# One GpSimd operation ahead of the weight-sum DMAs of a hybrid decoder layer

## The chip, the core and the metric

The kernel runs on one core of a Trainium2 chip. A core has five engines that run their own instruction streams and meet only at semaphores: TensorE (PE in the profile; its weight loads are PEld), VectorE (DVE), ScalarE (ACT), GpSimd (POOL) and SyncE (SP). DMAs are issued from the streams of SP, ACT and POOL, and all of them are carried out by the same 16 DMA engines. The metric is the device time of one execution in microseconds, as the median of three runs.

## The reference

The reference is one inference step of one decoder layer, for a prompt of 2048 tokens and for 8 samples of 8 tokens, in float32. Cut to what matters here:

```python
proj = einsum('btd,dp->btp', x, w_in)              # 1024 -> 3584: q, f, i, g, B, C, h
qh   = silu(q)
f    = lb + (1 - lb) * sigmoid(f_pre)              # forget gate;  k = 1 - f
o    = hgrn2(qh, log f, k, i)                      # gated linear recurrence, 4 heads of 128
o    = o * rsqrt(mean(o * o) + 1e-6) * onorm_g * silu(g)
yc   = B * conv3(C * h)
x    = layer_norm(alpha * x + concat(o, yc) @ w_out)
hid  = square(relu(x @ w_ff1))                     # 1024 -> 4096
x    = layer_norm(alpha * x + hid @ w_ff2)         # 4096 -> 1024
```

The outputs are the tokens after the second norm, the final states of the recurrence and the last two rows of the convolution's input, for prompt and samples.

## The kernel before

**Tiling.** The prompt is worked in four blocks of 512 tokens (`for b in range(NB)`); the samples ride along in the second block. Each block goes through the same stages: `m1` (the projections of q and f for the four heads, eight units), `m2` (i and g, eight units), `m3` (the convolution's three projections, twelve units), the output projection, the first norm, `ff1` and `ff2`. A unit is one weight tile of 128 x 1024 float32, 512 KB. Every float32 product is made of three fast matmuls: a high part and a low part of both operands are kept, and `mm3` (lines 230 to 232) issues high x high, high x low and low x high. A unit of `m1` on 512 columns is therefore 8 x 3 = 24 matmuls of 128x512.

**Weights.** All weight tiles of the whole run stand in one list (`units`) in the order of use. `unit_dma` (lines 171 and 173) issues the load of the next one from SP, into a `tok` buffer for the first six units and into one of three `st` buffers afterwards. `unit_split` makes the high part on ACT (line 194, or 155 for halves) and the low part on DVE (line 201 or 156). The block's input `x` comes through the same list. In the first block the list begins: first tile of q (unit 1's weights), four tiles of `x`, first tile of f (unit 2's weights), second tile of q (unit 3's weights), and so on, so unit 1 needs five tiles in SBUF and each later unit one more. Before the loop six loads are issued, then the small constants, then seven tiles are split.

**m1.** `main()` is a generator that yields twice per unit. Odd units give q. Even units give f and k: ACT takes the sigmoids out of PSUM (lines 433, 434) and scales them (435, 437); the results are `fs[h]` and `ks[h]`. With these, `head(h)` later works on DVE, and it overwrites `ks[h]` in place (line 585).

**The weight sums.** `ff2` uses a fast matrix multiplication scheme with seven products in place of eight. For that it needs four sums and differences of quarters of `w_ff2`, called T1 to T4, for each of eight chunks. They do not depend on the input, and they are built in DRAM by DMAs issued from POOL: `make_sums` yields 64 DMAs of 512 KB, 32 plain copies (line 331) and 32 accumulating ones (line 329, the destination is read, added to and written). Consecutive steps on the same chunk wait for the DMA before them; with eight chunks in turn, up to eight are in flight. The results are first read by the loads of `ff2` in the first block (`st<-T`). The loop that drives `main()` calls `making` twice per step from step 8 on, in the first block only.

**What sets the order.** The kernel fixes the program order itself, and each engine runs its own part of it in order. The position in the program is therefore not a time: an instruction runs as soon as its engine's earlier instructions have been issued and its semaphores are there. On POOL nothing stands ahead of the sums but three small memsets; behind them come the small power operations of the first block's norms (line 686 for the recurrence's outputs, line 262 for the layer norm).

Of the kernel before, what the change touches and what calls it, by code (L numbers as in the profile page):

```python
# [13 lines left out]
ALU = mybir.AluOpType  # L14
AX = mybir.AxisListType

P = 128
# [36 lines left out]
def hybrid_step(ctx, tc, a, o):  # L54
    nc = tc.nc
    v, s, g, te = nc.vector, nc.scalar, nc.gpsimd, nc.tensor
# [8 lines left out]
    def new(shape, tag, bufs, dt=F32, of=None):  # L65
        count[0] += 1
        return (of or pool).tile(list(shape), dt, tag=tag, bufs=bufs, name=f"{tag}{count[0]}")
# [26 lines left out]
    def SM(shape):  # L94
        return new(shape, "sm", 16)
# [129 lines left out]
    def pump():  # L225
        if bg:
            bg.pop(0)()
# [147 lines left out]
    for b in range(NB):  # L375
# [20 lines left out]
        qs, ks, fs, scs, kds = {}, {}, {}, {}, {}  # L396
# [421 lines left out]
        def rec_step():  # L818
            nonlocal rec_done
            if not rec_done:  # L820
                rec_done = next(rec, 0) == 0

        def main():
            yield from m1()
            yield from m2()
            yield from m3()

        for i, _ in enumerate(main()):
            rec_step()
            if b == 0 and i >= 8:  # L830
                next(making, 0)
                next(making, 0)
            if i >= 16 and i % (3 if samp else 4) == 0:
                rec_step()
            if i % 2 == 0:
                pump()
# [445 lines left out]
```

## Time and profile before

| | before |
|---|---|
| median of 3 runs | 2435.18 us (2433.24 to 2436.19) |
| profiled execution | 2430.45 us, of which the span is 2428.6 us |
| PE busy | 2393.4 us (99%) |
| DVE / ACT / POOL busy | 1535.9 us (63%) / 1115.1 us (46%) / 132.4 us (5%) |
| DMA, moved in all | 358.78 MB, mean 148 GB/s |
| queue q1 (issued from SP) | 313.88 MB, 39.5% of the 16 engines' time |
| queue q0 (issued from POOL) | 42.54 MB, 6.6% |

The span runs from the first to the last instruction; the time of an execution is 1.85 us longer in the profiled one. A busy PE is not a PE at its peak: a matmul's end is modelled, so the distance between the starts of matmuls says more than busy time does. "Landing" of a DMA is when its semaphore comes; an ACT or DVE instruction that waits for it starts right then, so its start tells when the tile landed. The DMA share is the mean busy share of the 16 engines and can read a little over 1.

### The profile page before, as it was taken

To read this page: it belongs to the slowest core of one execution; us is meant where nothing else is said; L and a number is where in the kernel's file an instruction comes from. 1 tells how busy PE (TensorE), PEld (TensorE's weight loads), DVE (VectorE), ACT (ScalarE), POOL (GpSimd) and SP (SyncE) were. 2 spreads that over 40 slices of the span, in tenths; PEclk is the share of its full clock that TensorE was granted. 3 is DMA by queue.
4 is the path that set the end of the run, shared out by engine and by line. 5 is a ranking of instruction groups with operands and counts; after the bars stand their busy time and mean duration, and the time that the engine had idled before them with its cause. 6 is when DMAs were issued, how large, how long until landed. Compare 5 with 4: busy or idle time off the path is not lost.

```text
span 2428.6 us, 32948 instructions
## 1 busy us (share of the span) xinstructions
PE 2393.4 (99%) x12876; PEld 2050.9 (84%) x12876; DVE 1535.9 (63%) x2370; ACT 1115.1 (46%) x1794; POOL 132.4 (5%) x159
## 2 busy tenths in 40 slices
PE   7999999999999999999999999999999999999998
PEld 5888988888889889997878888988887888988886
DVE  5756822787865684227778856623887865832787
ACT  4334644555324455445554244544555324644553
POOL 3210000000001110000000000000000000000001
PEclk9999999999999999999999999999999999999999
DMA  9984433566223733234453325423565324433563
GB/s 326 279 240 174 157 104 113 170 188 210 79 77 77 210 125 105 82 102 152 161 190 105 100 74 196 145 99 118 186 207 166 104 76 163 156 113 103 169 195 114
DMA packets 103547, 358.78 MB, mean 148 GB/s; under 512 B 11552, under 2 KB 16032, under 8 KB 103392
## 3 DMA queue, kind: packets, MB, share of 16 engines
q1 hardware_dynamic: 91216, 313.88, 39.5%
q0 software_dynamic: 12032, 42.54, 6.6%
q8 instruction: 101, 1.65, 0.3%
q14 instruction: 54, 0.44, 0.1%
q10 hardware_dynamic: 144, 0.26, 0.0%
HBM read 345.59 MB, written 44.60 MB: 161 GB/s over the span
## 4 chain that ended last, share of the span: by engine, by line
PE 49%; DVE 2%; DMA 1%; issue 0%; ACT 0%; ACTq 0%; DVEq 0%; SPq 0%
PE ps L230 11%; PE ps L232 10%; PE ps L231 10%; PE ps L238 5%; PE ps L236 5%; PE ps L237 5%; PE ps L654 1%; DMA st<-T 1%; DVE wl L201 1%; PE ps L241 0%; PE ps L242 0%; DMA st<-in_w_ff 0%; DVE tok L1081 0%; PE ps L743 0%; PE ps L740 0%
## 5 line engine op out<-in xcount | busy, mean ns | idle before, releaser
L201 DVE TENSOR_TENSOR wl<-st,wh 128x1024 fp32r<-128x1024 f32 x514 | 627.8, 1222 | 500.6 <-ACT wh L194 499.8
L230 PE MATMUL ps<-X,wh 128*128 128x512 f32 (+2 forms) x2272 | 778.2, 343 | 15.7 <-ACT X L155 12.4
L232 PE MATMUL ps<-X,wl 128*128 128x512 f32 (+2 forms) x2272 | 768.0, 338 | 1.1 <-DVE wl L201 1.1
L231 PE MATMUL ps<-X,wh 128*128 128x512 f32 (+2 forms) x2272 | 768.2, 338 | 0.3 <-DVE X L156 0.3
L194 ACT ACTIVATE wh<-st 128x1024 fp32r<-128x1024 f32 x515 | 543.3, 1055 | 370.6 <-PE ps L238 155.2
L230 PEld LDWEIGHTS ps<-X,wh 128*128 128x128 f32 x2272 | 430.5, 189 | 61.3 <-ACT X L155 14.0
L232 PEld LDWEIGHTS ps<-X,wl 128*128 128x128 f32 x2272 | 430.4, 189 | 43.7 <-DVE wl L201 1.9
L231 PEld LDWEIGHTS ps<-X,wh 128*128 128x128 f32 x2272 | 430.6, 190 | 41.8 <-DVE X L156 2.4
L238 PE MATMUL ps<-wh,l 128*128 128x512 f32 x868 | 340.3, 392 | 2.8 <-DVE l L156 2.3
L237 PE MATMUL ps<-wl,h 128*128 128x512 f32 x868 | 338.5, 390 | 0.6 <-DVE wl L201 0.6
L236 PE MATMUL ps<-wh,h 128*128 128x512 f32 x868 | 338.3, 390 | 0.0
L1011 ACT ACTIVATE raw<-ps 128x256 f32<-128x256 f32 (+1 forms) x184 | 85.7, 466 | 371.2 <-PE ps L232 369.4
L238 PEld LDWEIGHTS ps<-wh,l 128*128 128x128 f32 x868 | 163.1, 188 | 43.9 <-DVE l L156 10.5
L237 PEld LDWEIGHTS ps<-wl,h 128*128 128x128 f32 x868 | 163.1, 188 | 36.2 <-DVE wl L201 2.2
L236 PEld LDWEIGHTS ps<-wh,h 128*128 128x128 f32 x868 | 163.2, 188 | 33.3 <-ACT h L155 0.3
L156 DVE TENSOR_TENSOR l<-raw,h 128x512 fp32r<-128x512 f32 x217 | 148.5, 684 | 30.1 <-ACT h L155 30.1
L155 ACT ACTIVATE h<-raw 128x512 fp32r<-128x512 f32 x217 | 133.5, 615 | 3.7 <-PE ps L237 2.2
L262 POOL TENSOR_TENSOR sm<-sm,nhalf 128x1 f32<-128x1 f32 (+1 forms) x34 | 36.0, 1059 | 1705.2 <-DVE sm L261 1659.1
L230 PE MATMUL ps<-wh,X 128*128 128x512 f32 x256 | 104.0, 406 | 0.0
L230 PE MATMUL ps<-wh,S 128*128 128x512 f32 x256 | 101.3, 396 | 0.0
L232 PE MATMUL ps<-wh,X 128*128 128x512 f32 x256 | 100.3, 392 | 0.0
L232 PE MATMUL ps<-wh,S 128*128 128x512 f32 x256 | 100.0, 390 | 0.0
(202 smaller groups left out, 2474.0 us busy)
## 6 DMA issues: line engine op xcount, KB each, us to landing
st<-in_w_ff SPq DMA_DIRECT2D x249, 512.0 KB, 3.3
st<-T SPq DMA_DIRECT2D x124, 512.0 KB, 4.0
st<-in_w_in SPq DMA_DIRECT2D x110, 512.0 KB, 3.4
st<-in_w_out SPq DMA_DIRECT2D x56, 512.0 KB, 3.8
T<-in_w_ff POOLq DMA_DIRECT2D x48, 512.0 KB, 19.5
T<-T POOLq DMA_DIRECT2D x16, 512.0 KB, 19.0
lnb<-in_lnb SPq DMA_DIRECT2D x16, 512.0 KB, 5.7
tok<-in_x SPq DMA_DIRECT2D x16, 512.0 KB, 6.9
```

The lines of the kernel that those rows point to most:

```text
L155: s.activation(hi, src, AF.Copy)
L156: later.append(lambda: v.tensor_tensor(lo, src, hi.bitcast(F32), ALU.subtract))
L194: s.activation(wh, st, AF.Copy)
L201: v.tensor_tensor(wl, st, wh.bitcast(F32), ALU.subtract)
L230: te.matmul(out, lh, rh, start=first, stop=False)
L231: te.matmul(out, lh, rl, start=False, stop=False)
L232: te.matmul(out, ll, rh, start=False, stop=last)
L236: te.matmul(out, lh, rh, start=first, stop=False, skip_group_check=True)
L237: te.matmul(out, lh, rl, start=False, stop=False, skip_group_check=True)
L238: te.matmul(out, ll, rh, start=False, stop=last, skip_group_check=True)
L262: g.tensor_tensor(st[:n, 15:16], st[:n, 14:15], nhalf[:n, 0:1], ALU.pow)
L1011: s.activation(r[:, h0:h1], ps[:, :256 * (h1 - h0)].rearrange("p (s t) -> p s t", t=256), AF.Relu)
```

## The change

At step 6 of the first block's main loop (after step 6's work was put in the program, that is in the middle of the fourth unit), one GpSimd operation is inserted that adds one column of `ks[0]` and one column of `fs[0]`, the second unit's results, into a small tile that nothing reads. The calls of `making` now begin at step 6 instead of step 8, behind that operation.

```diff
         for i, _ in enumerate(main()):
             rec_step()
-            if b == 0 and i >= 8:
+            if b == 0 and i >= 6:
+                if i == 6:
+
+                    g.tensor_tensor(SM((P, 1)), ks[0][:, 0:1], fs[0][:, 0:1], ALU.add)
                 next(making, 0)
                 next(making, 0)
```

On POOL, before, the rows around the first sum DMAs (T_0_81 is the sum T1 of chunk 0, in_w_ff the weights):

```order
L126 MEMSET nhalf 128x4
L127 MEMSET halo 128x8
L128 MEMSET ones 128x128
L331 DMA T_0_81<-in_w_ff 128x1024
L331 DMA T_1_85<-in_w_ff 128x1024
L331 DMA T_2_89<-in_w_ff 128x1024
L331 DMA T_3_93<-in_w_ff 128x1024
```

On POOL, in the changed kernel, with what each row waits for (S_245 is `ks[0]`, S_244 is `fs[0]`, the semaphore is ACT's):

```order
L126 MEMSET nhalf 128x4
L127 MEMSET halo 128x8
L128 MEMSET ones 128x128
L833 ISA
L833 TENSOR_TENSOR sm_311<-S_245,S_244 128x1 [waits Activation_49]
L331 DMA T_0_81<-in_w_ff 128x1024
L331 DMA T_1_85<-in_w_ff 128x1024
L331 DMA T_2_89<-in_w_ff 128x1024
```

The first DMA had no wait ahead of it and now stands behind an operation that waits for ACT. The ISA row, which stood ahead of the first power operation (line 686) before, has moved up with the first arithmetic on POOL. The 64 DMAs keep their order, and the power operations still stand behind the last of them.

On DVE, in the changed kernel, where `head(0)` first overwrites q (S_205) and k (S_245) in place:

```order
L426 TENSOR_TENSOR S_281<-ps_256,S_282 128x512 [waits Activation_49]
L605 TENSOR_TENSOR S_333<-S_205,S_245 128x256 [waits DVE_49]
L611 TENSOR_TENSOR S_337<-S_286,S_288 128x512 [waits Activation_49]
L584 TENSOR_TENSOR S_205<-S_205,S_244 128x256 [waits DVE_49]
L585 TENSOR_TENSOR S_245<-S_245,S_244 128x256 [waits Pool_49]
L591 TENSOR_TENSOR S_285<-S_244 128x256
```

The order is that of before. New is the wait of the L585 row for POOL, since the inserted operation reads `ks[0]` before this row overwrites it.

## The prediction

> **What bounds the kernel now.** First the page, for the engine that is nearly always busy, and for what one load and one small POOL operation take:
>
> ```profile
> PE 2393.4 (99%) x12876; PEld 2050.9 (84%) x12876; DVE 1535.9 (63%) x2370; ACT 1115.1 (46%) x1794; POOL 132.4 (5%) x159
> ...
> L262 POOL TENSOR_TENSOR sm<-sm,nhalf 128x1 f32<-128x1 f32 (+1 forms) x34 | 36.0, 1059 | 1705.2 <-DVE sm L261 1659.1
> ...
> st<-in_w_ff SPq DMA_DIRECT2D x249, 512.0 KB, 3.3
> ```
>
> PE sets the time, so a change counts only where it removes PE's idle time or lets PE start sooner. PE's waits say where that is:
>
> ```profile
> PE ps L230 <- ACT X L155: 12.4, 3, 10.2
> PE ps L230 <- ACT wh L194: 2.8, 2, 2.1
> ```
>
> Both are in the opening of the first block. The timeline of that opening shows why (start, duration, engine, line; in brackets the idle time before and what ended it):
>
> ```profile
> 1.35 4.29 POOL L331 DMA_DIRECT2D T<-in_w_ff  x8 [0.34 <-issue]
> ...
> 3.57 0.63 ACT L155 ACTIVATE wh<-tok 128x512 fp32r<-128x512 f32 x1 [1.55 <-DMA tok<-in_w_in]
> ...
> 9.51 0.63 ACT L155 ACTIVATE X<-tok 128x512 fp32r<-128x512 f32 x1 [4.23 <-DMA tok<-in_xt]
> ...
> 10.19 0.79 PE L230 MATMUL ps<-X,wh 128*128 128x512 f32 x1 [10.19 <-ACT X L155]
> 10.92 0.79 PE L231 MATMUL ps<-X,wh 128*128 128x512 f32 x1
> ...
> 11.51 0.63 PE L232 MATMUL ps<-X,wl 128*128 128x512 f32 x1
> ...
> 14.62 0.80 PE L230 MATMUL ps<-X,wh 128*128 128x512 f32 x1 [0.58 <-ACT X L155]
> ...
> 18.98 1.15 ACT L155 ACTIVATE X<-tok 128x512 fp32r<-128x512 f32 x2 [1.39 <-DMA tok<-in_xt]
> ...
> 20.20 0.63 PE L230 MATMUL ps<-X,wh 128*128 128x512 f32 x1
> 20.63 0.52 PE L231 MATMUL ps<-X,wh 128*128 128x512 f32 x1
> ...
> 21.65 1.06 ACT L194 ACTIVATE wh<-tok 128x1024 fp32r<-128x1024 f32 x1 [1.52 <-DMA tok<-in_w_in]
> ...
> 30.31 1.06 ACT L194 ACTIVATE wh<-st 128x1024 fp32r<-128x1024 f32 x1 [7.61 <-DMA st<-in_w_in]
> ...
> 31.42 0.50 PE L230 MATMUL ps<-X,wh 128*128 128x512 f32 x1 [2.12 <-ACT wh L194]
> ...
> 37.59 0.39 PE L232 MATMUL ps<-X,wl 128*128 128x512 f32 x1
> 37.82 0.39 PE L230 MATMUL ps<-X,wh 128*128 128x512 f32 x1
> ```
>
> The eight first sum DMAs leave POOL at 1.35. The input's first quarter tile lands at 9.51, its last tile at 18.98, unit 2's weights at 21.65, unit 3's at 30.31, and PE waits for each. Unit 4 begins at 37.82, and from there to the output projection no row of PE's waits is left: PE then runs one matmul per 0.23 us. The opening is bound by loads, and the loads share the engines with the sums:
>
> ```profile
> core 0: us, PE busy (x) PEld busy (x) DVE busy (x) ACT busy (x) POOL busy (x), PEclk, DMA share, GB/s
> 2.00:3.00 1.00, 0.00 (x0) 0.00 (x0) 0.00 (x0) 0.02 (x1) 1.00 (x3) 1.00 0.92 299
> 197.00:203.00 6.00, 6.00 (x28) 4.97 (x27) 1.78 (x3) 1.55 (x2) 0.00 (x0) 1.00 1.00 388
> 4.00:20.00 16.00, 9.23 (x18) 5.49 (x19) 5.72 (x9) 5.41 (x10) 4.22 (x9) 1.00 1.01 388
> ...
> q0 software_dynamic: 971, 3.56, 57.8%
> q1 hardware_dynamic: 1003, 2.64, 43.2%
> ```
>
> The last two lines are the queues in 4 to 20 us: POOL's queue q0 has 57.8% of the engines' time, SP's q1 moves 2.64 MB in 16 us, 165 GB/s. In 197 to 203 us, a stretch after the sums, SP's loads have the engines to themselves and get 388 GB/s; in 2 to 3 us, before POOL's first packet, 299.
>
> **The change part by part.** *The hold.* The sums now start when ACT has written `ks[0]` (line 437) and POOL has run one more operation. Until then SP's loads are alone. I take 299 GB/s from 2 to 3 us, 388 after, and 0.65 us from the last byte to the landing (at 299 GB/s the first half weight tile, 0.26 MB, is moved by 2.9 and landed at 3.57). Bytes before each landing: the first quarter of x at 0.79 MB, x complete at 2.62 MB, unit 2's weights at 3.15 MB, unit 3's, with the constants of 0.31 MB ahead, at 3.98 MB. So they land at 3 + 0.49/0.388 + 0.65 = 4.9 (before 9.51), 3 + 2.32/0.388 + 0.65 = 9.6 (before 18.98), 11.0 (21.65) and 13.1 (30.31).
>
> *Unit 1.* PE starts 0.68 us after x's first landing (9.51 to 10.19): at 5.6. The first three matmuls keep the spacing of 10.19, 10.92, 11.51; from about 7.3 on the next part of x has landed and PE runs on without a gap. But PE is slow at first: 0.43 us from one matmul to the next (20.20, 20.63), which ends just after 20.63, though the granted clock column reads 1.00 there. That is 6.0 us after the last sizeable gap (14.62), or 4.7 us after unbroken work began around 15.94; I take 5.4, so the faster pace comes at 12.7. By then 3 + (12.7 - 7.3)/0.427 = 15.6 of 24 matmuls are done; the other 8.4 take 1.9 us. Unit 1 ends at 14.6. The last tile of x, landed at 9.6, is split by about 11.4 and doesn't hold it.
>
> [...]
>
> If instead it is a number of matmuls or time since the first one that counts, unit 1 stays slow: 7.3 + 21 x 0.427 = 16.3. That is the lower end of the gain. The upper end is x itself: split by 11.4 plus three matmuls, 12.1.
>
> *Units 2 and 3.* Their weights are split by 11.0 + 1.1 + 1.2 = 13.3 and 15.4, ahead of 14.6 and 20.1, so both run at 24 x 0.23 = 5.5 us: unit 2 to 20.1, unit 3 to 25.6. Unit 4 begins at 25.6 instead of 37.82: **12.2 us** sooner. With the ends above: 10.5 to 14.7.
>
> *The operation itself.* ACT's part between unit 2 and the hold:
>
> ```profile
> 36.89 0.58 ACT L433 ACTIVATE S<-ps 128x512 f32<-128x512 f32 x1
> ...
> 38.54 0.72 ACT L437 ACTIVATE S<-S,lw 128x512 f32<-128x512 f32 x1
> ...
> 45.42 0.42 DVE L585 TENSOR_TENSOR S<-S,S 128x256 f32<-128x256 f32 x1
> ```
>
> From 36.89 to 39.26 is 2.4 us, so `ks[0]` is there at 20.3 + 2.4 = 22.7, and with 1.06 us for a 128x1 operation the first DMA leaves at 23.8. The POOL operation costs no other engine time: DVE's L585, the only one that waits for it, runs 6.2 us after ACT's end (45.42 against 39.26), and needs it 1.1 us after. Without that cover it would cost 1.1 us.
>
> *The sums, later.* Their work is the same, only shifted. The queues in 0 to 40 us and in 40 to 170 us, then the landing of SP's loads from 37 to 170 us:
>
> ```profile
> q0 software_dynamic: 2392, 8.75, 59.9%
> ...
> q0 software_dynamic: 6804, 24.76, 81.0%
> q1 hardware_dynamic: 3031, 11.02, 22.4%
> ...
> DMA to landing us min/median/max: 5.2/8.0/11.8
> ```
>
> In all the sums take 0.599 x 40 + 0.81 x 130 = 129 us of all 16 engines. From 23.8, 1.7 us to the first packet (1.35 to about 3), and with SP taking its share 129/0.81 = 160 us: they end near 185 instead of 170, so their last issue moves from 147.82 to about 163. Loads beside them take 8.0 us instead of 3.3. PE had no wait with that before, from 37.82 on, at one load per 5.5 us and several tiles split ahead: no cost, and the pipeline is fuller when it begins. What stands behind the sums on POOL are the power operations:
>
> ```profile
> 147.82 0.81 POOL L329 DMA_DIRECT2D T<-in_w_ff  x1 [1.61 <-DMA T<-T]
> 173.60 1.88 POOL L686 TENSOR_TENSOR sm<-sm,nhalf 128x4 f32<-128x4 f32 x1 [24.96 <-DVE sm L685]
> ...
> 178.58 1.16 ACT L689 ACTIVATE S<-ps,sm 128x128 f32<-128x128 f32 x4
> ...
> 184.67 0.69 DVE L691 TENSOR_TENSOR S<-S,tok 128x512 f32<-128x512 f32 x1
> ...
> 188.19 1.13 PE L695 MATMUL ps<-ident,S 128*128 128x128 f32 x8
> ```
>
> The first was ready 25 us after the queue was free. Now it is due at 173.6 - 12.2 = 161.4, and POOL is free at about 164: 2.6 us late. Its result, ready at 175.5, was used by ACT only at 178.58 (3.1 us of room), and what ACT then makes (by 179.7) was used by DVE at 184.67 (5.0 more). So PE's L695 is reached only if POOL is over 8.1 us late. Cost: nothing, or one us per us beyond that. The sums are read much later:
>
> ```profile
> 404.14 11.20 SPq L173 DMA_DIRECT2D st<-T  x3
> ```
>
> Sum: 12.2 us less. The profiled execution would take 2430.45 - 12.2 = 2418.2; the median of the runs stands 4.73 above that execution, so I predict 2435.18 - 12.2 = **2423.0 us**. Nothing after the opening changes, so the whole shift should reach the end.
>
> **The rivals.** *A smaller relief.* SP's loads alone may not get 388 GB/s at the start: 299 in 2 to 3 us speaks for it, as does SP's own issue, whose first eight loads leave only by 6 us. At 299 throughout, unit 2's weights land at 13.2 instead of 11.0 and are split at 15.5; the loss is about 1 us. At 250 they land at 15.2 and unit 2 starts near 17.5, 3 us later: 9 us of gain. With a PE that stays slow for all of units 1 and 2 as well, 48 x 0.427 from 5.6 on, unit 3 starts at 26.5 and the gain is 12.2 - 6.4 = 5.8. So 5 to 10.5 us, 2425 to 2430.
>
> *The sums run late into the output projection (the other side).* That stage takes one tile per 2.7 us:
>
> ```profile
> 212.21 1.16 ACT L196 ACTIVATE wh<-st,small 128x1024 fp32r<-128x1024 f32 x1 [0.46 <-ACT wh L194]
> 214.95 1.15 ACT L196 ACTIVATE wh<-st,small 128x1024 fp32r<-128x1024 f32 x1 [1.59 <-PE ps L232]
> ```
>
> Three `st` buffers, each held for 8.0 us of loading and 2.4 of splitting beside the sums, give a tile per 3.5 us, 0.8 us too slow, 10.5 us over the stage's 14 tiles. With PE 12.2 us ahead the stage begins near 200, and it is hit if the sums end after that; I have 185. Past 200 the POOL queue is also 15 us later than I count, and the power operations cost 9 to 10 us. With both in full, 2435.2 - 12.2 + 10.5 + 10 = 2443. For this the sums would need 175 us and more where I count 160. The SP side is the same bytes in the same order, which speaks against it; an accumulating DMA that suffers more from loads than I assume speaks for it. In part it gives a result near 2435.
>
> *The hold frees nothing.* If the first landings are set by latency or by SP's own issue rather than by the shared engines, PE gains nothing, the sums start at 41 and end near 203, and the first power operation is 7.7 us late, within the room of 8.1: 2435. Against it: the share of 1.01 in 4 to 20 us.
>
> **How the numbers follow.** Forecast (10.5 to 14.7 us less) 0.68; smaller relief 0.16; sums late 0.10, half of it slower and half near the time before; nothing freed 0.06, of which 0.01 slower. A difference of 0.2% is 4.9 us, about what a measurement of this kernel can tell from no change. Faster: 0.68 + 0.16 = 0.84. Same: 0.05 + 0.05 = 0.10. Slower: 0.06. The forecast's own range is 2420.5 to 2424.7; with the spread of the runs (1.5 us each way) and the smaller relief the range is 2420 to 2430, which leaves out the last two rivals.
>
> **What would show it.** The first L331 on POOL at 22 to 26; x's first landing near 5, its last near 10; PE's first matmul at 5.6; the 2.1 us wait for L194 gone; unit 4's first matmul at 24 to 28 (the 73rd matmul on PE). Then no new row in PE's waits up to the output projection, the last L329 near 163, the first L686 waiting on POOL's own queue rather than on DVE. Wrong it is if the landings of x move by less than 4 us, if L695 or the output projection's first matmuls wait, or if the span shrinks by less than unit 4 moves.

## The result, and the profile after

The changed kernel takes 2419.91 us, median of 6 runs (2418.84 to 2424.68), against 2433.41 us for the kernel before, 6 runs on the same chip (2428.6 to 2436.19). The ratio is 0.995, with a 95% interval of 0.9938 to 0.9962: 9 to 15 us less, 12.2 us by the ratio. The profiled execution took 2419.32 us with a span of 2417.5 us, where before it was 2430.45 and 2428.6: 11.1 us less. The forecast was 2423.0 us, 12.2 us less; taken as a time, 2419.91 lies just under its range of 2420 to 2430.

PE's waits in the first 24 us of the changed kernel, and then from 24 to 600 us (total in us, times, longest):

```profile
PE ps L230 <- ACT X L155: 6.2, 2, 5.9
```

```profile
PE ps L238 <- DVE l L156: 0.6, 1, 0.6
PE ps L237 <- DVE wl L201: 0.2, 1, 0.2
```

The first wait for the input is 5.9 us long where it was 10.2, the 2.8 us for the weights of units 2 and 3 (0.7 and 2.1) are gone, and after the opening only the 0.6 us of the second view are new. The timeline of the opening (start, duration, engine, line; in brackets the idle time before and what ended it):

```profile
5.25 0.63 ACT L155 ACTIVATE X<-tok 128x512 fp32r<-128x512 f32 x1
5.93 0.79 PE L230 MATMUL ps<-X,wh 128*128 128x512 f32 x1 [5.93 <-ACT X L155]
...
7.46 0.63 ACT L155 ACTIVATE X<-tok 128x512 fp32r<-128x512 f32 x1 [1.58 <-DMA tok<-in_xt]
...
8.15 0.79 PE L230 MATMUL ps<-X,wh 128*128 128x512 f32 x1 [0.27 <-ACT X L155]
...
9.89 0.63 PE L230 MATMUL ps<-X,wh 128*128 128x512 f32 x1
...
11.41 1.15 ACT L155 ACTIVATE X<-tok 128x512 fp32r<-128x512 f32 x2 [0.18 <-DMA tok<-in_xt]
...
12.75 1.06 ACT L194 ACTIVATE wh<-tok 128x1024 fp32r<-128x1024 f32 x1 [0.19 <-DMA tok<-in_w_in]
13.79 0.63 PE L230 MATMUL ps<-X,wh 128*128 128x512 f32 x1
14.22 0.48 PE L231 MATMUL ps<-X,wh 128*128 128x512 f32 x1
14.54 0.40 PE L232 MATMUL ps<-X,wl 128*128 128x512 f32 x1
14.95 1.06 ACT L194 ACTIVATE wh<-st 128x1024 fp32r<-128x1024 f32 x1 [1.14 <-DMA st<-in_w_in]
...
16.14 0.39 PE L230 MATMUL ps<-X,wh 128*128 128x512 f32 x1
...
24.26 0.69 POOL L833 TENSOR_TENSOR sm<-S,S 128x1 f32<-128x1 f32 x1 [23.24 <-ACT S L437]
24.90 4.31 POOL L331 DMA_DIRECT2D T<-in_w_ff  x8
27.02 0.39 PE L230 MATMUL ps<-X,wh 128*128 128x512 f32 x1
```

The inserted operation (L833) runs at 24.26, and the first sum DMAs leave behind it at 24.90 instead of 1.35. Until then the loads are alone. The first half of the input's first tile has landed at 5.25 (before 9.51; the prediction calls it a quarter, but with four tiles it is an eighth of the input), the last tile at 11.41 (18.98), unit 2's weights at 12.75 (21.65), unit 3's at 14.95 (30.31). PE's spacing changes from 0.43 to 0.23 us near 14.4. Unit 2 starts at 16.14, and unit 4 at 27.02 instead of 37.82: 10.8 us sooner, which is the 11.1 us of the span within 0.3.

What the opening costs in bytes, by windows (us, engines, granted clock, DMA share, GB/s):

```profile
core 0: us, PE busy (x) PEld busy (x) DVE busy (x) ACT busy (x) POOL busy (x), PEclk, DMA share, GB/s
2.00:3.00 1.00, 0.00 (x0) 0.00 (x0) 0.00 (x0) 0.02 (x1) 0.00 (x0) 1.00 0.85 260
3.00:11.00 8.00, 4.80 (x9) 2.58 (x10) 4.28 (x7) 4.59 (x8) 0.00 (x0) 1.00 0.99 372
36.00:170.00 134.00, 134.00 (x757) 112.07 (x756) 90.35 (x198) 44.55 (x79) 39.54 (x56) 1.00 1.04 289
```

The third row is the stretch in which the sums now run: PE is busy in all of its 134 us, with 757 matmuls. Where the sums end on POOL:

```profile
162.38 0.81 POOL L329 DMA_DIRECT2D T<-in_w_ff  x1 [0.59 <-DMA T<-T]
162.93 1.74 POOL L686 TENSOR_TENSOR sm<-sm,nhalf 128x4 f32<-128x4 f32 x1
...
167.78 1.16 ACT L689 ACTIVATE S<-ps,sm 128x128 f32<-128x128 f32 x4
...
177.39 1.13 PE L695 MATMUL ps<-ident,S 128*128 128x128 f32 x8
```

The last sum DMA leaves at 162.38 (before 147.82), and the first power operation (L686) stands right behind it at 162.93 with no idle time in between. Before, it came 25 us after the queue was free. ACT's L689 and PE's L695 run 10.8 us sooner than before (178.58 and 188.19), so nothing of the 10.8 us is lost there.

### The profile page after: what moved, and what is told of

Same layout as the page of the kernel before. It is cut to its first block, busy times and chain, and to the rows that moved or that the text cites. A ratio compares the mean times of both kernels' runs of the same rounds, so it can differ in the third digit from the quotient of the medians.

```text
span 2417.5 us, 32951 instructions
## 1 busy us (share of the span) xinstructions
PE 2390.5 (99%) x12876; PEld 2051.4 (85%) x12876; DVE 1536.2 (64%) x2370; ACT 1114.6 (46%) x1794; POOL 131.6 (5%) x160
## 4 chain that ended last, share of the span: by engine, by line
PE 50%; DVE 2%; DMA 1%; issue 0%; ACT 0%; DVEq 0%; ACTq 0%
PE ps L230 11%; PE ps L232 10%; PE ps L231 10%; PE ps L238 5%; PE ps L237 5%; PE ps L236 5%; PE ps L654 1%; PE ps L241 0%; PE ps L242 0%; DVE wl L201 0%; PE ps L743 0%; PE ps L740 0%; PE ps L712 0%; PE ps L870 0%; DVE l L156 0%
```

## The experiments

The theory has three steps: the sums share the DMA engines with the first loads; holding them back lets PE start sooner by about 11 us; the sums then run under a PE that waits for nothing, and only their end, ahead of the power operations, has a limit. The rivals were that the operation itself or the earlier calls of `making` do it, that the accumulating DMAs rather than the plain copies are in the way, and that the late sums cost something that a milder hold would give back. All kernels below are edits of the changed kernel. The kernel before was run again beside them, with medians of 2432.14, 2432.18 and 2432.07 us, and the ratios are to these.

**Is it the hold?** In the first kernel the operation is taken out, and the calls still begin at step 6:

```diff
-                if i == 6:
-                    g.tensor_tensor(SM((P, 1)), ks[0][:, 0:1], fs[0][:, 0:1], ALU.add)
```

> Only the operation is taken out; the calls that make the sums still begin at step 6. Shared engines (the sums take half of the DMA engines from the opening loads): the first sum DMA leaves POOL at 1.35 again, x is complete near 19, unit 4 begins at 37.8, the time is that of the kernel before, 2433 within 3 us. Rival (the earlier place in the program, or POOL's instruction load that moved up, is what helped): unit 4 begins near 27 and the time is near 2420.

Measured: 2431.83 us (10 runs), ratio 0.9997 (0.9988 to 1.0006). The timeline of its opening:

```profile
1.35 4.29 POOL L331 DMA_DIRECT2D T<-in_w_ff  x8 [0.34 <-issue]
...
18.29 1.15 ACT L155 ACTIVATE X<-tok 128x512 fp32r<-128x512 f32 x2 [1.37 <-DMA tok<-in_xt]
...
30.43 0.50 PE L230 MATMUL ps<-X,wh 128*128 128x512 f32 x1 [1.96 <-ACT wh L194]
...
38.32 0.39 PE L230 MATMUL ps<-X,wh 128*128 128x512 f32 x1
```

The DMAs leave at 1.35 again, the input is complete at 18.29, the wait for unit 3's weights is back, and unit 4 begins at 38.32. The step at which `making` is called counts for nothing without the wait. (The next kernel keeps the operation and lets DMAs go ahead of it, so it tells whether the operation alone does anything.)

**Which DMAs?** The sums begin with plain copies into the sum buffers; the accumulating DMAs follow. Here the 16 copies go ahead of the operation, and only the accumulating DMAs behind it:

```diff
                 if i == 6:
+                    for _ in range(2 * NCH):
+                        next(making, 0)
                     g.tensor_tensor(SM((P, 1)), ks[0][:, 0:1], fs[0][:, 0:1], ALU.add)
```

> The 16 first plain copies stand ahead of the operation, only what follows, with all accumulating DMAs, stands behind it. Shared engines: the copies alone fill POOL's queue until about 41, so the opening is that of the kernel before, unit 4 at 37.8, time 2433 within 3 us. Rival (it is the accumulating DMAs that harm the loads): unit 4 near 27 to 30 and 2420 to 2425.

Measured: 2433.05 us (10 runs), ratio 1.000 (0.9991 to 1.001). Its timeline:

```profile
37.62 0.39 PE L230 MATMUL ps<-X,wh 128*128 128x512 f32 x1
37.89 0.69 POOL L834 TENSOR_TENSOR sm<-S,S 128x1 f32<-128x1 f32 x1 [13.76 <-ACT S L437]
38.53 6.75 POOL L329 DMA_DIRECT2D T<-in_w_ff  x8
```

Not one accumulating DMA leaves before 38.53, and unit 4 still begins at 37.62, as before the change. The copies alone undo the whole gain, with the operation in place: what matters is that POOL's DMAs run beside the first loads, not that they accumulate. With 4 copies ahead instead of 16 the effect should come in part:

> Four of the plain copies stand ahead of the operation, the other 60 sum DMAs behind it. Theory (what the opening loses is the engine time of the sum bytes moved beside the loads, 512 KB at 388 GB/s = 1.35 us each): while the four copies last, the loads get half, so x's last tile lands 4 x 1.35 = 5.4 us later than 11.4, at about 17, unit 1 ends near 19, unit 4 begins near 30.4, between 27.0 and 37.8; time about 2423 to 2424. Rival (any sum DMA in the opening disturbs it as much as all): 36 to 38, 2431 to 2433. Rival (four are swallowed by the room in front of unit 3): 27, 2420.

```profile
1.35 2.26 POOL L331 DMA_DIRECT2D T<-in_w_ff  x4 [0.33 <-issue]
...
31.39 0.39 PE L230 MATMUL ps<-X,wh 128*128 128x512 f32 x1
```

Measured: 2425.2 us (6 runs), ratio 0.9973 (0.9961 to 0.9985). Unit 4 begins at 31.39: with no copies ahead it is 27.02, with four 31.39, with all 37.62. About 1.1 us per 0.5 MB of copy for the first four: four copies are 2.1 MB, for which the engines need 5.6 us at the 372 GB/s of the opening, and 4.4 of them came through to PE. That is 1.0 us more than was expected for unit 4, and the time is 1.2 us above the expected range. Whether the copies take the loads' place at the engines themselves or at the memory behind them, these runs don't separate.

**How long must the hold be?** Here the operation reads the last tile of the input instead of the second unit's results:

```diff
-                    g.tensor_tensor(SM((P, 1)), ks[0][:, 0:1], fs[0][:, 0:1], ALU.add)
+                    z = xh[KT - 1][:, TB - 1:TB].bitcast(F32)
+                    g.tensor_tensor(SM((P, 1)), z, z, ALU.add)
```

> The operation reads the last tile of x instead of the second unit's results, so the sums start near 14 instead of 24.9. Theory (only the loads up to unit 3's weights set PE's opening, the later ones have 10 us of room): unit 4 begins at 27.0 as in the changed kernel, give or take 0.5, the sums end 10 us earlier (last issue near 151), time 2420 within 3 us. Rival (every load that meets the sums in the opening costs PE time): unit 4 2 to 4 us later, 2422 to 2424.

```profile
12.59 0.19 POOL L833 TENSOR_TENSOR sm<-X 128x1 f32<-128x1 f32 x1 [11.57 <-ACT X L155]
12.72 4.32 POOL L331 DMA_DIRECT2D T<-in_w_ff  x8
26.75 0.39 PE L230 MATMUL ps<-X,wh 128*128 128x512 f32 x1
...
152.10 0.81 POOL L329 DMA_DIRECT2D T<-in_w_ff  x1 [0.42 <-DMA T<-T]
162.52 1.88 POOL L686 TENSOR_TENSOR sm<-sm,nhalf 128x4 f32<-128x4 f32 x1 [9.61 <-DVE sm L685]
```

Measured: 2419.97 us (4 runs), ratio 0.9949 (0.9934 to 0.9964): the same as the change, with the sums 12 us sooner on their way. Unit 4 begins at 26.75. The loads of units 2 and 3 were far enough ahead by 12.7, so the last 12 us of the hold buy nothing that can be seen. They cost nothing either, but POOL is now free 9.61 us before the first power operation instead of 0.

**And if it is too long?** The operation reads the results of a later head, so that the sums end later. First the second head's (the calls begin at step 7), then the fourth's (at step 15, with all 64 DMAs right behind):

```diff
-            if b == 0 and i >= 6:
-                if i == 6:
-                    g.tensor_tensor(SM((P, 1)), ks[0][:, 0:1], fs[0][:, 0:1], ALU.add)
+            if b == 0 and i >= 7:
+                if i == 7:
+                    g.tensor_tensor(SM((P, 1)), ks[1][:, 0:1], fs[1][:, 0:1], ALU.add)
```

> The operation reads the second head's f and k (unit 4) instead of the first head's, so the sums start near 36, 11 us later. Theory of the room behind the sums (8.1 us before PE is reached by a late power operation): the last sum issue moves to about 174, the first power operation comes about 11 us late, PE's line 695 waits about 3 us, time about 2423. Rival (more cover than counted): no wait, 2420. Rival (a late power operation also blocks ACT's queue, weights and PSUM): 5 to 10 us of PE idle, 2425 to 2430.

```diff
-            if b == 0 and i >= 6:
-                if i == 6:
-                    g.tensor_tensor(SM((P, 1)), ks[0][:, 0:1], fs[0][:, 0:1], ALU.add)
-                next(making, 0)
-                next(making, 0)
+            if b == 0 and i == 15:
+                g.tensor_tensor(SM((P, 1)), ks[3][:, 0:1], fs[3][:, 0:1], ALU.add)
+                for _ in making:
+                    pass
```

> The operation reads the fourth head's f and k (unit 8), so the sums start near 57, 32 us later than in the changed kernel. Theory of the room behind the sums (8.1 us, then one us per us): the last issue is near 195, the first power operation 32 us late, PE loses about 24 us near line 695, the output projection starts after the sums have ended and loses nothing more: about 2444, slower than the kernel before. Rival (the sums overlap the output projection and the power operations don't matter): PE's waits are for split weights in the output projection, up to 10 us, 2425 to 2430. Rival (cover is much larger): 2420.

Measured: 2425.8 us for the second head (9 runs, 2418.42 to 2427.79; ratio 0.997, 0.996 to 0.998) and 2446.25 us for the fourth (4 runs; ratio 1.0057, 1.0043 to 1.007), so slower than before the change. The timeline of the second head's kernel:

```profile
174.68 2.33 POOL L686 TENSOR_TENSOR sm<-sm,nhalf 128x4 f32<-128x4 f32 x2
...
177.99 0.66 PE L695 MATMUL ps<-ident,S 128*128 128x128 f32 x4 [1.38 <-DVE S L691]
181.67 1.11 PE L695 MATMUL ps<-ident,S 128*128 128x128 f32 x4 [3.03 <-DVE S L691]
...
187.01 0.60 PE L695 MATMUL ps<-ident,S 128*128 128x128 f32 x4
```

and two windows of it:

```profile
179.30:186.20 6.90, 4.53 (x13) 3.76 (x14) 3.05 (x6) 5.59 (x22) 2.14 (x2) 0.51 1.06 242
906.20:909.70 3.50, 3.50 (x16) 3.50 (x15) 1.96 (x3) 0.00 (x0) 0.00 (x0) 0.53 0.00 0
```

The first power operation runs at 174.68. Without sums it is ready at 161.41 (the kernel without sums, below), and unit 4 began 0.43 us later here (26.08 against 25.65), so it is due at 161.8 and 12.9 us late. PE waits 1.38 + 3.03 = 4.4 us: the room is 8.5 us. The granted clock is then 0.51 for 6.9 us, which no expectation had. PE works in 4.53 us of these and waits in the rest, so by estimate the slow clock costs about 2.3 us besides, half of the 4.53. Unit 4 began 0.9 us sooner than in the changed kernel, and the row at 187.01 stands 5.9 us later than there (181.13): 4.4 + 2.3 - 0.9 = 5.8. The span is 8.5 us longer. Another 1.7 us come at 906, where the clock falls once more for 3.4 us (the second window), in a stretch that has nothing to do with the sums and in which it stayed up in the changed kernel; 0.9 us are left over. The wait was expected as 3 us and the time as 2423. The time of 2425.8 lies in the range of the rival that had PE idle for 5 to 10 us, but PE idled for 4.4, and the slow clock makes up most of the rest. One of the nine runs took 2418.42: its mean granted clock is 0.999, that of the other eight 0.996 to 0.998, so in this run the clock stayed up nearly all the time (0.003 of 2420 us is 7 us).

The fourth head's kernel, by its timeline and then by PE's waits from 30 to 300 us:

```profile
194.56 2.33 POOL L686 TENSOR_TENSOR sm<-sm,nhalf 128x4 f32<-128x4 f32 x2
```

```profile
PE ps L695 <- DVE S L691: 24.4, 2, 21.8
```

Due at 161.3, run at 194.56: 33.3 us late, 24.4 us of waiting, room 8.9 us. That is one us per us beyond the room, as counted. These 24.4 us are PE's only wait in that stretch. (Here too the granted clock is down behind the first of the two waits, 0.50 from 199.0 to 206.5.) The output projection didn't meet the sums even here: the wait put PE off too, and the first of its split rows that the prediction quoted (ACT's line 196, at 212.21 before) comes at 227.4, behind the sums' last landing at 215.8.

**What do the sums cost once they run?** Here the operation and the calls are removed, and the second matrix is read from raw quarters in place of the sums T1 to T4, so this kernel leaves the sums out of the computation:

```diff
-        return a["w_ff2"][c * 4 + RAW[k]] if k in RAW else sums[c][k]
+        return a["w_ff2"][c * 4 + RAW.get(k, SUMS.index(k) if k in SUMS else 0)]
```

> The weight sums are left out altogether, with the operation: the loads of the second half of the feed-forward stage read raw quarters in place of T1 to T4, so that stage computes something else, on the same number of bytes. Theory (after the opening the sums are fully hidden): unit 4 at 27.0 and a time equal to the changed kernel's, 2420 within 2 us. Rival (their DMAs still cost PE time between 25 and 190, by slower loads): 2410 to 2417.

```profile
36.00:170.00 134.00, 134.00 (x758) 112.09 (x757) 89.00 (x195) 44.76 (x85) 2.88 (x2) 1.00 0.21 75
```

Measured: 2420.89 us (4 runs), ratio 0.9951 (0.9936 to 0.9966): no faster than the changed kernel. The window shows why. The DMA share falls from 1.04 to 0.21 and PE, which was busy for 134.00 of 134 us with the sums, is busy for 134.00 without them, with 758 matmuls against 757. After the change the sums cost nothing that can be measured. The spans alone would mislead: unit 4 begins 1.4 us sooner here (25.65), and the span is 2.3 us longer. Of these 3.7 us about 3.4 are two stretches of 3.4 us at half clock that the changed kernel doesn't have (0.51 from 897.2 to 900.7, and 6.9 us instead of 3.4 us near 1140).

**Is PE's slow pace in unit 1 the rest?** The changed kernel runs the first 16 of unit 1's 24 matmuls 0.43 us apart or more. Two kernels keep PE busy before the input lands, on a piece of memory set to 1.0 (the first with 11 small matmuls ahead of the loads, the second with the same 11 and then 7 and 2 more behind the first two steps of unit 1):

```diff
+    v.memset(lnb[:, 0, :P], 1.0)
+    wps = PS()
+    for _ in range(11):
+        te.matmul(wps[:, :P], lnb[:, 0, :P], lnb[:, 0, :P], start=True, stop=True)
     def load_constants():
```

> The changed kernel, with eleven small matmuls on a constant tile ahead of the loads, so that PE is at work from about 1 to 5.9 us, before x lands; their result is read by nobody. Theory (PE's slow pace ends after some 5 us of unbroken work, whatever the matmuls): unit 1 runs at 0.23 us per matmul and is then bound by x's last tile (landed at 11.4, split by 13.4), unit 4 begins near 25.0 instead of 27.0, time about 2418. Rival (the slow pace hangs on the number of large matmuls or on time alone): unit 4 at 27.0, 2420.

Measured: 2419.76 us (5 runs), ratio 0.9946 (0.9933 to 0.9958). The timeline (each of the 11 stands as two rows) and two windows:

```profile
1.06 4.37 PE L124 MATMUL ps<-lnb 128*128 128x128 f32 x22 [1.06 <-DVE lnb L121]
...
7.61 0.52 PE L235 MATMUL ps<-X,wh 128*128 128x512 f32 x1 [2.18 <-ACT X L160]
...
25.95 0.39 PE L235 MATMUL ps<-X,wh 128*128 128x512 f32 x1
```

```profile
4.50:8.00 3.50, 1.32 (x9) 0.92 (x8) 1.41 (x3) 1.28 (x3) 0.00 (x0) 0.99 0.87 314
8.00:11.40 3.40, 3.19 (x8) 2.48 (x8) 2.82 (x5) 2.55 (x5) 0.00 (x0) 0.50 1.03 404
```

PE's pace rose near 4.5, 3.4 us after the first small matmul at 1.06 where some 5 were expected (4 or 5 rows of the small matmuls per half microsecond from 1.5 to 4.5, 6 from there to 5.0), though the granted clock reads 1.00 from 0.5 to 4.5 as well. After a wait of 2.18 us for the input the clock was down at 0.50 from 8.0 to 11.4. Unit 4 begins at 25.95 where 25.0 was expected: a miss. With the gaps filled:

```diff
+                if u == 0 and k < 2:
+                    fill((7, 2)[k])
```

> The warmed kernel with nine more small matmuls in the two gaps in which PE waits for x in unit 1, so that it never rests. Theory (the clock falls back for 3.4 us after a window with idle time in it): the granted clock goes up near 4.5 and stays up, unit 1 is bound by x's last tile and ends near 14, unit 4 begins at 25.0 give or take 0.4; time 2418 to 2419, which the runs can hardly tell from 2420. Rival (the fall-back is not caused by the gap): clock half again in 6 to 12, unit 4 at 26 to 27.

Here `fill(n)` stands for n of the small matmuls. The 3.4 us and the window with idle time in it are those of the kernel with 11 matmuls: PE busy for 1.32 of the 3.50 us from 4.5 to 8.0, then 3.4 us at 0.50. Measured: 2419.8 us (5 runs), ratio 0.9951 (0.9938 to 0.9963). The same window, and the timeline:

```profile
8.00:11.40 3.40, 3.40 (x24) 3.07 (x23) 2.55 (x4) 2.33 (x5) 0.00 (x0) 1.00 1.03 400
```

```profile
14.07 0.39 PE L241 MATMUL ps<-X,wl 128*128 128x512 f32 x1
...
15.22 0.50 PE L241 MATMUL ps<-X,wl 128*128 128x512 f32 x1 [0.31 <-DVE wl L210]
...
25.83 0.39 PE L239 MATMUL ps<-X,wh 128*128 128x512 f32 x1
```

The clock now stays at 1.00 in that window, and unit 1's last matmul starts at 14.07 instead of 15.92. But unit 2 then waits for the low part of its weights (the row at 15.22), and unit 4 begins at 25.83: a miss again, by 0.8 us against 25.0. Against the changed kernel that is 1.2 us in the profile, and nothing that the times can tell. Nor are the 1.2 us surely the small matmuls' doing: the kernels that hold for the second and the fourth head and the one without sums, none of them warmed, begin unit 4 at 26.08, 25.50 and 25.65. None of the kernels is measurably faster than the changed one.

## Why the prediction was right, step by step

**The bound.** It was the opening, and the sums' share of the engines in it. Without the hold the whole gain is gone (2431.83 us), and with the copies alone let through it is gone too (2433.05). The rival that the hold frees nothing is out.

**The landings.** Counted 4.9, 9.6, 11.0 and 13.1, landed by 5.25, 11.41, 12.75 and 14.95. The first is right, the others are 1.8 us late. The rates explain a part: with 260 GB/s in 2 to 3 us and 372 after, in place of 299 and 388, the last tile of the input is through when 2.62 MB are, and lands at 3 + 2.36/0.372 + 0.65 = 10.0, so 0.4 of the 1.8. The other 1.4 us are there already with the second half tile: it lands at 7.46, 2.2 us after the first, and from 8.80 on each tile takes 1.3 us (0.52 MB at 400 GB/s). Either the lag from the last byte to the landing is longer than the 0.65 us taken from a single early load, or bytes of later loads went ahead; no run here tells which.

**Unit 1.** This is the mis-sized term: it was to end at 14.6, and unit 2 starts at 16.14, 1.5 us later. Two parts of the step failed. Its first six matmuls took until 9.89, where 5.6 + 1.7 + 3 x 0.427 = 8.6 was counted: PE began 0.33 us late, the fourth matmul came 0.5 us late on top of it because of the input, and the second three came as slowly as the first. At 0.43 us a matmul from there to a change of pace at 12.7, and 0.23 after, the unit would have ended at 15.3. And the change of pace came near 14.4 instead of 12.7, for the other 0.8 us. This second part scatters: in the kernels that hold for the input, for the second and the fourth head, and that leave the sums out, unit 2 starts at 15.87, 15.20, 14.62 and 14.19, so the counted 14.6 was in reach. Nor did the last tile of the input become the bound when the pace was mended: the kernel with the filled gaps ran into unit 2's weights instead.

**Units 2 and 3.** Right: 16.14 to 27.02 is 10.9 us for 48 matmuls, where 11.0 was counted, with no wait. Unit 4 is 10.8 us sooner instead of 12.2, inside the range of 10.5 to 14.7 given for the step.

**The operation and its place.** Counted first DMA at 23.8, seen at 24.90, later by the 1.5 us of unit 1, less 0.4 because the operation took 0.69 us where 1.06 was taken; neither time has anyone waiting for it.

**The shift of the sums.** Right: the last issue at 162.38 (counted 163), the last landing at 186.4 (counted 185), 161.5 us after the first issue, where 1.7 + 160 was counted. The rival that they last 175 us is out. The first power operation was to be 2.6 us late and was not late at all, since PE came 1.4 us later and POOL was free at 162.9 instead of 164. The room of 8.1 us is shown: 8.5 and 8.9 us by the two kernels with longer holds.

**The other side.** The late sums do have a price, 24.4 us of waiting at 33.3 us late, but by the power operations. The first half of the rival, loads of the output projection that suffer from the sums, was reached in no run: when the sums run so late, PE waits at L695 and the projection moves back with it. Its price, 10.5 us, remains untested, and the two halves could not have come in full together as the rival's 2443 has it.

**The sum.** 12.2 us were counted from the opening, 10.8 came from it, and the span is 11.1 us shorter. The change of the medians is larger than that of the two profiled executions (13.5 against 11.1). Beside the later runs of the kernel before, whose medians are near 2432.1, kernels of the same opening stand 12 us lower. That the ratio gives the very 12.2 us of the forecast is in part luck: its interval of 9 to 15 us doesn't tell 10.8 from 12.2, and in the profiled execution unit 1 ended 1.5 us later than counted. The time of 2423.0 was 3.1 us too high: 1.8 us because it started from the median of 3 runs, 2435.18, where 6 runs give 2433.41, and the rest is the difference between 12.2 and 13.5.

## What to carry to other kernels

In the kernel before, background DMAs that waited for nothing started at 1.35 us and took 57.8% of the engines' time from 4 to 20 us, while the first loads decided when the main engine started. An operation of their own queue that reads something the first loads produce held them back here at no cost that could be seen, and the hold needed to last only until the input was there: here 12.7 us served as well as 24.9. How far the hold could go was set by what stands behind the background work on the same queue: a room of 8.5 to 8.9 us, and beyond it about a microsecond per microsecond (4.4 us of waiting at 12.9 us late, 24.4 at 33.3). So count that room first.

## What the hardware showed that was not expected

**The clock fell after short waits.** A wait of 2.18 us in the kernel with 11 matmuls ahead (PE busy 1.32 of 3.50 us, granted clock 0.99) was followed by 3.4 us at 0.50. With the same stretch filled, the clock stayed at 1.00. After 1.38 and 3.03 us of waiting in the second head's kernel it was 0.51 for 6.9 us. The kernel without the operation shows it too, after its 1.96 us wait for unit 3's weights:

```profile
31.50:34.90 3.40, 3.21 (x8) 2.54 (x9) 2.96 (x9) 2.94 (x4) 1.09 (x2) 0.50 1.02 418
```

The stretches at half clock are 3.4 us long, or 6.9 us, about twice that; what sets these lengths was not shown. Nor does a wait of some 2 us always bring one: the kernel before had a 2.12 us wait at the same place as the 1.96 us one and went on at full pace (0.23 us a matmul, granted clock 1.00 from 31 to 35). Likewise PE waits 3.3 us near 1140 in the kernel before, in the changed one and in the one that holds for the input, and the clock falls behind it in the first two (0.50 from 1148 to 1150 in the kernel before, 0.51 from 1137.3 to 1140.8 in the changed one) but not in the third (1.00 from 1130 to 1150, and no fall up to 2396). What decides between them stays open. Each fall of 3.4 us costs about 1.7 us, an estimate from the half clock, which bears on how runs of one kernel differ, as in the run of 2418.42 us above.

**When the pace first rises.** By the spacing of the matmuls the pace changed at 20.9 in the kernel before, at 14.4 in the changed one, at 13.2, 12.1, 12.0 and 9.8 in the kernels that hold for the input, for the second and the fourth head, and that leave the sums out, whose input lands within about 1 us of each other. The five spread over 4.6 us. The input's landing can make up about 1 us of that; where the rest comes from was not shown. A microsecond of it is worth about half a microsecond of time, an estimate from 0.23 against 0.43 us a matmul, so up to some 2 us between runs may come from it.
